# Position numbers behind a low part, five rows and three v tiles in flight, 33 u tiles ahead

## The chip, the cores and the metric

The kernel runs on one core of one Trainium2 chip. The metric is the device time of one execution in microseconds. Before the change it took 2081.49 us (median of 3 runs, 2076.62 to 2083.87).

## The reference

One layer each of two blocks over 512 tokens of width 1024, in float32. The first block (gated attention beside a gated delta rule) and the token mixers of the second (a linear recurrence beside a convolution) end at about 800 us of the profile and are not touched by the change. What the change touches is the last part, a product-key expert layer:

```python
q = (t @ w_q).reshape(n_tok, 8, 2, 128)              # 8 heads, 2 halves
sc = einsum("thpk,hpnk->thpn", q, sub_keys)           # 128 keys a half
s_top, i_top = top_k(sc, 16)                          # of each half
cand = s_top[:,:,0,:,None] + s_top[:,:,1,None,:]      # 16 x 16 pairs
best, pos = top_k(cand, 16); idx = cand_idx[pos]      # 16 experts a head
g = softmax(best)
act = gelu(einsum("phkd,pd->phk", u_tab[idx], t))     # 128 experts a token
out = einsum("phk,phkd->pd", g * act, v_tab[idx])     # of 16384 in the tables
```

The result is added to the residual, and a last rms norm follows.

## The kernel before, in words

Tokens stand on columns (512 of them) in the transposed layout, weights come as 128 x 1024 tiles. Float32 precision is had from pairs: a tile is cast to a rounded high part by ScalarE (`whi`, `vhi`, `xhi`, line 192) and the rest, the low part, is a subtraction on GpSimd or VectorE (`wlo`, `vlo`, `xlo`, line 193). Each product is three matmuls: high with high, low with high, high with low.

**Query stage** (`peer_query`). For each of 8 heads, two blocks of `wq` (one for each half, e = 0 and 1) are projected, scored against the keys (`scp`), and VectorE finds the 16 best of each half (`top16`, lines 1153 to 1157: `val`, `ind`). From the two sets of indices GpSimd makes the position numbers `f` (line 1054 from half 0, line 1055 from half 1), from them the candidates' indices `cidx` (line 1070); VectorE finds the 16 best pairs; then VectorE writes four masks `eq`, GpSimd multiplies each with `cidx` (`pr`, line 1096), and VectorE adds up (`idxf`, line 1097). Between the heads stand u tiles (`u_step`, line 988): two after each of the first seven heads and six after the last.

**u tiles and v tiles.** For 352 of the 512 tokens all 16384 experts are computed, 128 at a time. A u tile is 24 matmuls (`ups`), and its gelu is kept in a ring of `RUN` = 32 tiles (`act`). The v tile of the same number (18 matmuls into `acc`) comes `LAG` = RUN - 2 u tiles later, after the gate matrix (`gate_matrix`: one-hot matmuls `gp`, written to device memory as `gd`, read back as `gate` for four tiles at a time) has been multiplied into it (`act`, line 1317) and the product split into `ch` and `cl`. From u tile 20 on VectorE makes the low part of u; it makes those of v too.

**Rows.** The other 160 tokens gather their experts' rows: GpSimd issues an indirect DMA (line 1227) into one of `NROW` = 4 row buffers, and VectorE multiplies and sums each (lines 1233 and 1249). There are 160 rows of u and 160 of v, each 128 x 1024. They are paced by `spent`: 8 for each turn in which both a u and a v tile are done, 4 for a turn with a v tile alone, 324 steps over `total - 40`.

**What sets the order.** Instructions are recorded in the order of the code, and a scheduler puts them into each engine's queue; an engine then works through its queue in order. `tc.issue_after(ins)` holds the instructions of its block that are on `ins`'s engine behind `ins`. `vring` holds 4 v tiles in the buffer that was `xr`, which is free after its transposes into `acc` (line 1283). All loads but the rows go through SyncE's queue in order.

Of the kernel before, what the change touches and what calls it, by code (L numbers as in the profile page):

```python
# [6 lines left out]
F32 = mybir.dt.float32  # L7
# [5 lines left out]
OP = mybir.AluOpType  # L13
# [170 lines left out]
def vec(g, name, i, n=1):  # L184
    o, w = VEC[name]
    return g.vec[:, o + i:o + i + n]
# [15 lines left out]
def wblock(g, src, k=KD, width=128, lo_eng=None, ret=False, raw=None):  # L202
    nc = g.nc
    if raw is None:
        raw = wblock_load(g, src, k, width)
    hi = g.wp.tile([128, k, width], F32R, name="whi", tag="whi")
    lo = g.wp.tile([128, k, width], F32R, name="wlo", tag="wlo")
    last = split(g, hi, lo, raw, lo_eng or nc.gpsimd)
    return (hi, lo, last) if ret else (hi, lo)
# [15 lines left out]
def proj_tile(g, w, xhi, xlo, ks=range(KD), ps=None):  # L225

    if ps is None:
        ps = g.pmm.tile([128, 512], F32, name="mm", tag="mm")
    hi, lo = w
    mm3(g, ps, lambda k: hi[:, k, :], lambda k: lo[:, k, :], lambda k: xhi[:, k, :], lambda k: xlo[:, k, :], ks)  # L230
    return ps
# [744 lines left out]
TB = 32  # L976
GPAD = 128
NEXP = 128
RUN = 32
GB = 4  # L980
ULO = 20
NROW = 4
SMH = 4
UQ = [2, 2, 2, 2, 2, 2, 2, 6]
PM = 2


# [15 lines left out]
def peer_query(g, xr):  # L1003

    nc, tc = g.nc, g.tc
    V = nc.vector
    L = g.L
# [2 lines left out]
    g.xtok = {tt: L.tile([128, 1024], F32, name=f"xtok{tt}") for tt in GT}  # L1010
    g.xnt = {tt: L.tile([128, 1024], F32, name=f"xnt{tt}", tag=f"xnt{tt}") for tt in GT}
    g.xnx = L.tile([128, 1024], F32, name="xnx", tag="xnx")
    g.idxf = L.tile([128, 4, 128], F32, name="idxf")
    g.wgt = L.tile([128, 4, 128], F32, name="wgt")
    with ExitStack() as c2:
        P = c2.enter_context(tc.tile_pool(name="pq", bufs=1, reuse_waits="tile"))
        R = c2.enter_context(tc.tile_pool(name="pqr", bufs=2, reuse_waits="tile"))
# [9 lines left out]
        nx = P.tile([128, KD, len(DT) * 128], F32, name="nx")  # L1027
        for k in range(KD):
            V.scalar_tensor_tensor(nx[:, k, :], xr[:, k, cs], vec(g, "n2", k), g.rb[:, cs], op0=OP.mult, op1=OP.mult)
        for h in range(8):  # L1030
            val = R.tile([128, 4, 2, 16], F32, name="val")
            ind = R.tile([128, 4, 2, 16], U32, name="ind")
            for e in range(2):
                hp = 2 * h + e
                ps = proj_tile(g, wblock(g, g.a["wq"][hp]), g.xhi, g.xlo)
                if hp == 1:
                    for k in range(KD):
                        split(g, g.xhi[:, k, cs], g.xlo[:, k, cs], nx[:, k, :])
                qT = R.tile([128, T], F32, name="qT")
                nc.scalar.copy(qT, ps)  # L1040
                ps = pt.tile([128, 512], F32, name="scp", tag="pg")
                for tt in range(4):
                    nc.tensor.matmul(ps[:, tt * 128:(tt + 1) * 128], qT[:, tt * 128:(tt + 1) * 128], sk[:, hp, :],
                                     start=True, stop=True)
                sc = R.tile([128, 4, 128], F32, name="sc")
                for tt in range(4) if h == 0 else GT:
                    nc.scalar.activation(sc[:, tt, :], ps[:, tt * 128:(tt + 1) * 128], AF.Copy, scale=g.rtok[:, tt:tt + 1])
                if h:
                    nc.scalar.copy(sc[:, DT[0]:, :], ps.rearrange("p (t n) -> p t n", t=4)[:, DT[0]:, :])
                for tt in range(4):  # L1050
                    top16(g, R, val[:, tt, e, :], ind[:, tt, e, :], sc[:, tt, :])

            f = R.tile([128, 4, 2, 16], F32, name="f")
            nc.gpsimd.tensor_scalar(out=f[:, :, 0, :], in0=ind[:, :, 0, :], scalar1=128.0, scalar2=None, op0=OP.mult)
            nc.gpsimd.tensor_copy(f[:, :, 1, :], ind[:, :, 1, :])
            cand = R.tile([128, 4, NCAND], F32, name="cand")
            cidx = R.tile([128, 4, NCAND], F32, name="cidx")

            def pairs(eng, out, x, y, at, a, b, na, nb):

                o = out[:, :, at:at + na * nb]
                x, y = x[:, :, a:a + na], y[:, :, b:b + nb]
                if na > 1 and nb > 1:
                    s4 = [128, 4, na, nb]
                    o, x, y = o.rearrange("p t (a b) -> p t a b", b=nb), x[:, :, :, None].to_broadcast(s4), y[:, :, None, :].to_broadcast(s4)
                elif nb > 1:
                    x = x.to_broadcast([128, 4, nb])
                elif na > 1:
                    y = y.to_broadcast([128, 4, na])
                eng.tensor_tensor(out=o, in0=x, in1=y, op=OP.add)  # L1070

            for a in range(5):
                pairs(V, cand, val[:, :, 0, :], val[:, :, 1, :], START[a], a, 0, 1, START[a + 1] - START[a])
            pairs(V, cand, val[:, :, 0, :], val[:, :, 1, :], START[5], 5, 0, 3, 2)
            pairs(V, cand, val[:, :, 0, :], val[:, :, 1, :], START[8], 8, 0, 8, 1)
            at = 0
            for a, b, na, nb in RUNS:
                pairs(nc.gpsimd, cidx, f[:, :, 0, :], f[:, :, 1, :], at, a, b, na, nb)
                at += na * nb
            best = R.tile([128, 4, 16], F32, name="best")  # L1080
            pos = R.tile([128, 4, 16], U32, name="pos")
            for tt in range(4):
                top16(g, R, best[:, tt, :], pos[:, tt, :], cand[:, tt, :])
            pf = R.tile([128, 4, 16], F32, name="pf")
            V.tensor_copy(pf, pos)
            V.tensor_tensor(out=g.wgt[:, :, h * 16:h * 16 + 16], in0=best, in1=best[:, :, 0:1].to_broadcast([128, 4, 16]),
                            op=OP.subtract)
            for q, n in enumerate(ENDS):

                v4 = lambda t: t[:, :16 * n].rearrange("p (t k c) -> p t k c", t=4, k=4)  # L1090
                s4 = [128, 4, 4, n]
                eq = v4(R.tile([128, 16 * NCAND], BF16, name="eq"))
                V.tensor_tensor(out=eq, in0=rank[:, None, None, :n].to_broadcast(s4),
                                in1=pf[:, :, 4 * q:4 * q + 4, None].to_broadcast(s4), op=OP.is_equal)
                pr = v4(R.tile([128, 16 * NCAND], F32, name="pr"))
                nc.gpsimd.tensor_tensor(out=pr, in0=eq, in1=cidx[:, :, None, :n].to_broadcast(s4), op=OP.mult)  # L1096
                V.tensor_reduce(out=g.idxf[:, :, h * 16 + 4 * q:h * 16 + 4 * q + 4], in_=pr, axis=AX.X, op=OP.add)
            if h % SMH == SMH - 1:
                e = g.wgt[:, :, (h + 1 - SMH) * 16:(h + 1) * 16]
                e4 = e.rearrange("p t (h k) -> p t h k", k=16)  # L1100
                nc.scalar.activation(e, e, AF.Exp)
                l = R.tile([128, 4, SMH], F32, name="l")
                V.tensor_reduce(out=l, in_=e4, axis=AX.X, op=OP.add)
                V.reciprocal(l, l)
                V.tensor_tensor(out=e4, in0=e4, in1=l[:, :, :, None].to_broadcast([128, 4, SMH, 16]), op=OP.mult)
            for _ in range(UQ[h]):
                u_step(g)
        g.u_last = g.u_mm
        for n in range(0, KD, 4):
            for tt in GT:  # L1110
# [90 lines left out]
def peer_experts(g, out, xr, gd):  # L1201
    nc, tc = g.nc, g.tc
    V = nc.vector
    NB = ND // TB
    with ExitStack() as ctx:
# [16 lines left out]
        gx.dot = P.tile([128, GX], F32, name="dotx")  # L1222
        gat.insert(0, gx)

        def gather(s, tab, i):
            r = R.tile([128, 1024], F32, name="row", bufs=NROW)
            nc.gpsimd.indirect_dma_start(out=r, out_offset=None, in_=g.a[tab],  # L1227
                                         in_offset=bass.IndirectOffsetOnAxis(ap=s.idx[:, i:i + 1], axis=0))
            return r
# [26 lines left out]
        def finish(hs, tt):  # L1256

            ss = R.tile([128, 2], F32, name="ss")
            o = R.tile([128, 1024], F32, name="o", tag="row", bufs=NROW)
            half = [slice(e * 512, (e + 1) * 512) for e in range(2)]  # L1260
            sq = g.wp.tile([128, KD, 128], F32, name="wraw", tag="wraw").rearrange("p k d -> p (k d)")
            for e in range(2):
# [18 lines left out]
        for m, tt in enumerate(DT):  # L1281
            for k in range(KD):
                nc.tensor.matmul(acc[m][k // 4][:, (k % 4) * 128:(k % 4 + 1) * 128], xr[:, k, tt * 128:(tt + 1) * 128], g.ident,
                                 start=k % 4 == 0, stop=False)
        vring = g.xp.tile([128, 4, 1024], F32, name="vring", tag="xr")
        LAG = RUN - 2

        chl = [[P.tile([128, GX + ND], F32R, name=f"{n}{j}") for n in ("ch", "cl")] for j in range(2)]
# [12 lines left out]
                        nc.tensor.matmul(acc[m][e], l[:, ts], r[:, e * 512:(e + 1) * 512], start=False, stop=end and l is cl)  # L1301

        gt = None
        total = sum(8 if LAG <= n < NEXP else 4 for n in range(LAG, NEXP + LAG))
        spent = 0
        for n in range(NEXP + LAG):
            if n < NEXP:
# [10 lines left out]
                            in1=gt[:, :, i % GI, :], op=OP.mult)  # L1318
            ch, cl = chl[i % 2]
            split(g, ch[:, GX:], cl[:, GX:], act)  # L1320
            vr = vring[:, i % 4, :]
            nc.sync.dma_start(vr, g.a["v"][i * 128:(i + 1) * 128, :])
            vh = R.tile([128, 1024], F32R, name="vhi")
            vl = R.tile([128, 1024], F32R, name="vlo")
# [9 lines left out]
                    products([m])  # L1334
            if i != NEXP - 2:
                late.clear()
            spent += 8 if n < NEXP else 4
            with tc.issue_after(last.ins):
                while done < min(len(steps), len(steps) * spent // (total - 40)):
                    f, s, i = steps[done]  # L1340
# [41 lines left out]
```

## Time and profile before

| | |
|---|---|
| profiled execution | 2073.55 us |
| its span, first to last instruction | 2071.8 us |
| median of 3 runs | 2081.49 us |
| TensorE (PE) busy | 1992.9 us, 96% |
| VectorE (DVE) busy | 1554.4 us, 75% |
| GpSimd (POOL) busy | 1028.6 us, 50% |
| ScalarE (ACT) busy | 838.0 us, 40% |
| DMA | 423.43 MB, 204 GB/s over the span |

A share of busy time is a mean over stages. In the profile's 40 slices the DMA engines are in the nines from slice 23 on (about 1140 us), where u tiles, v tiles and rows run together, and low before. Idle time of TensorE is 78.9 us of the span in all; where it lies, and what ended it, is what has to be read.

### The profile page before, as it was taken

To read this page: it belongs to the slowest core of one execution; us is meant where nothing else is said; L and a number is where in the kernel's file an instruction comes from. 1 tells how busy PE (TensorE), PEld (TensorE's weight loads), DVE (VectorE), ACT (ScalarE), POOL (GpSimd) and SP (SyncE) were. 2 spreads that over 40 slices of the span, in tenths; PEclk is the share of its full clock that TensorE was granted. 3 is DMA by queue.
4 is the path that set the end of the run, shared out by engine and by line. 5 is a ranking of instruction groups with operands and counts; after the bars stand their busy time and mean duration, and the time that the engine had idled before them with its cause. 6 is when DMAs were issued, how large, how long until landed. Compare 5 with 4: busy or idle time off the path is not lost.

```text
span 2071.8 us, 28916 instructions
## 1 busy us (share of the span) xinstructions
PE 1992.9 (96%) x10588; PEld 1722.8 (83%) x10588; DVE 1554.4 (75%) x2647; ACT 838.0 (40%) x1337; POOL 1028.6 (50%) x876
## 2 busy tenths in 40 slices
PE   9999999899999999988999898999999999999997
PEld 6787887677888877877899787899989898989885
DVE  6635545367777778888898789898888888888683
ACT  5444444444444444333454333333333333333343
POOL 3544352345666555667677454454444444545330
PEclk9999999999999999999999999999999999999999
DMA  4111121312222233222366999999999999998682
GB/s 163 55 38 42 67 77 51 102 63 91 92 90 93 92 99 105 89 85 92 112 245 264 375 356 362 374 383 375 347 358 359 347 353 359 340 367 314 231 286 81
DMA packets 152125, 423.43 MB, mean 204 GB/s; under 512 B 12592, under 2 KB 57776, under 8 KB 150320
## 3 DMA queue, kind: packets, MB, share of 16 engines
q1 hardware_dynamic: 105904, 253.80, 35.1%
q0 software_dynamic: 46080, 167.79, 22.2%
q8 instruction: 83, 1.36, 0.3%
q14 instruction: 58, 0.48, 0.1%
HBM read 396.38 MB, written 25.17 MB: 203 GB/s over the span
## 4 chain that ended last, share of the span: by engine, by line
PE 42%; DVE 8%; issue 4%; POOL 4%; DMA 3%; ACT 0%; SPq 0%; POOLq 0%; DVEq 0%; ACTq 0%
PE acc L1301 22%; PE ups L217 16%; PE gp L1195 2%; POOL row L1227 2%; DMA gate<-gd 1%; PE mm L217 1%; DVE oh L1189 1%; DVE t L1155 1%; POOL pr L1096 1%; DMA row<-v,ix 1%; DVE ind L1154 1%; DVE ind L1157 1%; POOL oh L1191 1%; DVE val L1153 1%; DVE val L1156 1%
## 5 line engine op out<-in xcount | busy, mean ns | idle before, releaser
L193 POOL TENSOR_TENSOR wlo<-wraw,whi 128x1024 fp32r<-128x1024 f32 x136 | 334.9, 2467 | 219.4 <-ACT whi L192 215.8
L192 ACT CAST whi<-wraw 128x1024 fp32r<-128x1024 f32 x248 | 258.8, 1044 | 88.4 <-issue 31.8
L1227 POOL DMA_INDIRECT row<-v,idx x128 | 166.4, 1300 | 191.7 <-DVE xtok L1249 167.6
L1301 PE MATMUL acc<-vlo,ch 128*128 128x512 f32 x768 | 240.3, 393 | 9.6 <-DVE vlo L193 9.5
L1227 POOL DMA_INDIRECT row<-u,idx x128 | 157.7, 1232 | 179.1 <-DVE row L1233 163.4
L1301 PE MATMUL acc<-vhi,ch 128*128 128x512 f32 x768 | 240.2, 393 | 3.9 <-ACT ch L192 3.9
L1301 PE MATMUL acc<-vhi,cl 128*128 128x512 f32 x768 | 240.3, 394 | 0.0
L217 PE MATMUL mm<-xhi,wlo 128*128 128x512 f32 x824 | 221.4, 399 | 8.7 <-POOL wlo L193 8.7
L217 PE MATMUL mm<-xhi,whi 128*128 128x512 f32 x824 | 221.9, 402 | 4.3 <-DVE bb L863 3.7
L217 PE MATMUL mm<-xlo,whi 128*128 128x512 f32 x824 | 220.1, 399 | 0.0
L217 PE MATMUL ups<-xhi,whi 128*128 128x352 f32 x1024 | 197.2, 327 | 1.2 <-ACT act L999 1.2
L217 PE MATMUL ups<-xhi,wlo 128*128 128x352 f32 x1024 | 190.9, 326 | 7.2 <-POOL wlo L193 5.0
L217 PE MATMUL ups<-xlo,whi 128*128 128x352 f32 x1024 | 193.3, 327 | 1.7 <-DVE xlo L193 1.6
L192 ACT CAST ch<-act 128x352 fp32r<-128x352 f32 x128 | 62.4, 487 | 319.3 <-PE acc L1301 280.1
L999 ACT ACTIVATE act<-ups 128x352 f32<-128x352 f32 x128 | 59.4, 464 | 307.6 <-PE ups L217 307.6
L217 PEld LDWEIGHTS mm<-xhi,wlo 128*128 128x128 f32 x824 | 150.5, 189 | 39.4 <-POOL wlo L193 11.2
L1301 PEld LDWEIGHTS acc<-vlo,ch 128*128 128x128 f32 x768 | 144.0, 188 | 45.5 <-DVE vlo L193 13.9
L217 PEld LDWEIGHTS mm<-xhi,whi 128*128 128x128 f32 x824 | 148.9, 189 | 37.1 <-issue 9.2
L217 PEld LDWEIGHTS ups<-xhi,whi 128*128 128x128 f32 x1024 | 170.2, 189 | 11.2 <-ACT act L999 1.5
L217 PEld LDWEIGHTS mm<-xlo,whi 128*128 128x128 f32 x824 | 151.5, 189 | 30.8 <-issue 2.1
L217 PEld LDWEIGHTS ups<-xhi,wlo 128*128 128x128 f32 x1024 | 168.1, 190 | 9.2 <-POOL wlo L193 6.5
L1249 DVE SCALAR_TENSOR_TENSOR xtok<-row,dot,xtok 128x1024 f32<-128x1024 f32 x128 | 163.9, 1280 | 13.0 <-DMA row<-v,idx 11.5
(642 smaller groups left out, 3740.5 us busy)
## 6 DMA issues: line engine op xcount, KB each, us to landing
wraw<-uT SPq DMA_DIRECT2D x128, 512.0 KB, 6.5
vring<-v SPq DMA_DIRECT2D x128, 512.0 KB, 6.8
wraw<-w SPq DMA_DIRECT2D x88, 512.0 KB, 3.4
gd<-stage SPq DMA_DIRECT2D x11, 2048.0 KB, 7.2
gate<-gd SPq DMA_DIRECT2D x32, 704.0 KB, 9.4
wraw<-wo SPq DMA_DIRECT2D x16, 512.0 KB, 3.4
wraw<-wq SPq DMA_DIRECT2D x16, 512.0 KB, 3.5
xr<-xT SPq DMA_DIRECT2D x8, 256.0 KB, 6.6
```

Source lines behind the costliest of these rows:

```text
L192: nc.scalar.copy(hi, src)
L193: return (lo_eng or nc.vector).tensor_tensor(out=lo, in0=src, in1=hi.bitcast(F32), op=OP.subtract)
L217: yield nc.tensor.matmul(out, w(k), x(k), start=j == 0, stop=j == len(ps) - 1)
L999: nc.scalar.activation(act, ups, AF.Gelu_apprx_tanh)
L1096: nc.gpsimd.tensor_tensor(out=pr, in0=eq, in1=cidx[:, :, None, :n].to_broadcast(s4), op=OP.mult)
L1153: V.max(out=v[:, 0:8], in_=x)
L1154: V.max_index(out=i[:, 0:8], in_max=v[:, 0:8], in_values=x)
L1155: V.match_replace(out=y[:, :n], in_to_replace=v[:, 0:8], in_values=x, imm_value=-3.0e38)
L1195: nc.tensor.matmul(ps[:, j * 128:(j + 1) * 128], oh[:, 1, j, :], oh[:, 0, j, :], start=True, stop=True)
L1227: nc.gpsimd.indirect_dma_start(out=r, out_offset=None, in_=g.a[tab], in_offset=bass.IndirectOffsetOnAxis(ap=s.idx[:, i:i + 1], axis=0))
L1249: V.scalar_tensor_tensor(s.acc, r, s.dot[:, i:i + 1], s.acc, op0=OP.mult, op1=OP.add)
L1301: nc.tensor.matmul(acc[m][e], l[:, ts], r[:, e * 512:(e + 1) * 512], start=False, stop=end and l is cl)
```

## The change

Five things change together. The u tiles of a head and the next head's first `wq` block now stand in the code ahead of the position numbers, and these are held behind the last low part among them. There are five row buffers: four tiles of their own and the fourth slot of `vring`, so that the v tiles have three slots. The ring of u tiles has 33 places, for which `idxf` has moved into another buffer. The pace is 0 in the first two turns with a v tile.

```diff
-RUN = 32
+RUN = 33
+VR = 3
...
-NROW = 4
+NROW = 5
...
-UQ = [2, 2, 2, 2, 2, 2, 2, 6]
+UQ = [2, 2, 2, 2, 2, 2, 2, 3]
+UEND = 3
...
-    g.idxf = L.tile([128, 4, 128], F32, name="idxf")
+    g.idxf = g.hp.tile([128, 4, 128], F32, name="idxf", tag="rb")
...
+        wq = [wblock(g, g.a["wq"][0], ret=True)]
...
-                ps = proj_tile(g, wblock(g, g.a["wq"][hp]), g.xhi, g.xlo)
+                ps = proj_tile(g, (wq.pop(0) if wq else wblock(g, g.a["wq"][hp], ret=True))[:2], g.xhi, g.xlo)
...
+            for _ in range(UQ[h]):
+                last = u_step(g)
+            if h < 7:
+                wq.append(wblock(g, g.a["wq"][2 * h + 2], ret=True))
+                last = wq[0][2]
...
-            nc.gpsimd.tensor_scalar(out=f[:, :, 0, :], in0=ind[:, :, 0, :], scalar1=128.0, scalar2=None, op0=OP.mult)
-            nc.gpsimd.tensor_copy(f[:, :, 1, :], ind[:, :, 1, :])
+            with tc.issue_after(last.ins):
+
+                nc.gpsimd.tensor_scalar(out=f[:, :, 0, :], in0=ind[:, :, 0, :], scalar1=128.0, scalar2=None, op0=OP.mult)
+                nc.gpsimd.tensor_copy(f[:, :, 1, :], ind[:, :, 1, :])
...
-            for _ in range(UQ[h]):
-                u_step(g)
+        for _ in range(UEND):
+            u_step(g)
...
+        vring = []
+        rows = [P.tile([128, 1024], F32, name=f"row{j}") for j in range(NROW - 1)]
+        turn = [0]
+
+        def row():
+            turn[0] += 1
+            return (rows + [vring[0][:, VR, :]])[turn[0] % NROW]
+
         def gather(s, tab, i):
-            r = R.tile([128, 1024], F32, name="row", bufs=NROW)
+            r = row()
...
-        vring = g.xp.tile([128, 4, 1024], F32, name="vring", tag="xr")
+        vring.append(g.xp.tile([128, VR + 1, 1024], F32, name="vring", tag="xr"))
...
-        total = sum(8 if LAG <= n < NEXP else 4 for n in range(LAG, NEXP + LAG))
+        pace = lambda n: 0 if n < LAG + 2 else 8 if n < NEXP else 4
+        total = sum(map(pace, range(LAG, NEXP + LAG)))
...
-            vr = vring[:, i % 4, :]
+            vr = vring[0][:, i % VR, :]
...
-            spent += 8 if n < NEXP else 4
+            spent += pace(n)
```

GpSimd's queue at the third head's position numbers, before (`wlo` are low parts of weight blocks: the last of a head's two u tiles, then the next head's two `wq` blocks):

```order
L1096 TENSOR_TENSOR pr<-eq,cidx 128x800
L193 TENSOR_TENSOR wlo<-wraw,whi 128x1024
L1054 TENSOR_SCALAR f<-ind 128x4x16
L193 TENSOR_TENSOR wlo<-wraw,whi 128x1024 x2
L1055 CAST f<-ind 128x4x16
L1070 TENSOR_TENSOR cidx<-f 128x4x4
```

The same place of the changed kernel:

```order
L1106 TENSOR_TENSOR pr<-eq,cidx 128x800
L193 TENSOR_TENSOR wlo<-wraw,whi 128x1024 x2
L1064 TENSOR_SCALAR f<-ind 128x4x16
L193 TENSOR_TENSOR wlo<-wraw,whi 128x1024
L1065 CAST f<-ind 128x4x16
L1080 TENSOR_TENSOR cidx<-f 128x4x4
```

One low part, that of the next head's first `wq` block, now stands ahead of `f`. The low part of the last u tile ahead of it still stands behind the head's largest `pr`. At the other heads but the first it is the same move; no other engine's queue changes in this stage.

TensorE's queue where the first v tile begins, before (`acc` are the v tiles' sums; u tile 32 is the one that is split):

```order
L217 MATMUL ups<-xhi,whi 128x352 x8
L217 MATMUL ups<-xhi,wlo 128x352 x6
L1301 MATMUL acc_9676<-vhi,ch_9707 128x512
L1301 MATMUL acc_9677<-vhi,ch_9707 128x512
L1301 MATMUL acc_9676<-vlo,ch_9707 128x512
```

And now:

```order
L217 MATMUL ups<-xhi,whi 128x352 x8
L217 MATMUL ups<-xhi,wlo 128x352
L1319 MATMUL acc_9680<-vhi,ch_9711 128x512
L1319 MATMUL acc_9681<-vhi,ch_9711 128x512
L1319 MATMUL acc_9680<-vlo,ch_9711 128x512
```

The first v tile begins five u matmuls earlier, inside the same u tile. Before, v tiles 0 and 1 followed on each other there; now the rest of u tile 32 stands between them, and from v tile 2 on each v tile k has 32 + k whole u tiles ahead of it, where it had 31 + k.

VectorE's queue from the low part of v tile 10 to that of v tile 11, before (`row` and `accx` rows are gathered rows):

```order
L193 TENSOR_TENSOR vlo<-vring,vhi 128x1024
L1237 TENSOR_TENSOR dotx<-dotx,wx 128x32
L1241 MEMSET accx 128x1024
L1317 TENSOR_TENSOR act<-act,gate 128x352
L1249 SCALAR_TENSOR_TENSOR accx<-row,dotx,accx 128x1024
L193 TENSOR_TENSOR wlo<-wraw,whi 128x1024
L1249 SCALAR_TENSOR_TENSOR accx<-row,dotx,accx 128x1024
L1317 TENSOR_TENSOR act<-act,gate 128x352
L193 TENSOR_TENSOR cl_9710<-act,ch_9709 128x352
L1249 SCALAR_TENSOR_TENSOR accx<-row,dotx,accx 128x1024
L193 TENSOR_TENSOR vlo<-vring,vhi 128x1024
```

And now:

```order
L193 TENSOR_TENSOR vlo<-vring,vhi 128x1024
L1251 SCALAR_TENSOR_TENSOR row_9676,dotx<-row_9676,xnx 128x1024
L1336 TENSOR_TENSOR act<-act,gate 128x352 x5
L193 TENSOR_TENSOR wlo<-wraw,whi 128x1024
L1251 SCALAR_TENSOR_TENSOR row_9677,dotx<-row_9677,xnx 128x1024
L1251 SCALAR_TENSOR_TENSOR row_9678,dotx<-row_9678,xnx 128x1024
L193 TENSOR_TENSOR cl_9714<-act,ch_9713 128x352
L193 TENSOR_TENSOR vlo<-vring,vhi 128x1024
```

The gate products that run ahead of the v tiles have moved forward: counted from the first, 29 stand ahead of the low part of v tile 11 now, 13 before, beside 32 rows now and 35 before. The fifth of the five in one row is the first that needs the next gate block.

## Rows read from the trace of the kernel before

**Rows 1.** Busy time of engines by stretch: PE, PEld, DVE, ACT, POOL, PEclk, DMA, GB/s.

```profile
1133.00:1340.00 207.00, 191.33 (x976) 167.54 (x975) 171.66 (x234) 70.12 (x102) 95.22 (x71) 0.98 1.02 367
1340.00:2057.00 717.00, 717.00 (x3687) 639.04 (x3686) 595.70 (x741) 264.16 (x369) 308.08 (x247) 1.00 0.91 326
```

**Rows 2.** Waits of TensorE from 800 to 1012 us: total, times, longest.

```profile
PE mm L217 <- POOL wlo L193: 8.7, 6, 1.9
PE ups L217 <- POOL wlo L193: 5.0, 5, 2.4
```

**Rows 3.** Timeline of GpSimd from 848 us: start, us, instruction, idle before.

```profile
852.32 2.42 POOL L193 TENSOR_TENSOR wlo<-wraw,whi 128x1024 fp32r<-128x1024 f32 x1
858.58 0.37 POOL L1054 TENSOR_SCALAR f<-ind 128x64 f32<-128x64 uint32 x1 [3.85 <-DVE ind L1157]
858.92 4.72 POOL L193 TENSOR_TENSOR wlo<-wraw,whi 128x1024 fp32r<-128x1024 f32 x2
...
875.71 2.41 POOL L193 TENSOR_TENSOR wlo<-wraw,whi 128x1024 fp32r<-128x1024 f32 x1
```

**Rows 4.** Timeline of TensorE from 848 us.

```profile
878.17 1.54 PE L217 MATMUL ups<-xhi,wlo 128*128 128x352 f32 x8 [0.21 <-POOL wlo L193]
...
884.68 2.85 PE L217 MATMUL mm<-xhi,wlo 128*128 128x512 f32 x8 [1.87 <-POOL wlo L193]
```

**Rows 5.** Waits of TensorE from 1133 to 1340 us.

```profile
PE acc L1301 <- DVE vlo L193: 9.5, 7, 2.2
PE acc L1301 <- ACT ch L192: 3.9, 1, 3.9
PE ups L217 <- DVE wlo L193: 2.1, 1, 2.1
```

**Rows 6.** Chain that ended last, 1120 to 1140 us: start, us, piece.

```profile
1127.62 9.96 DMA gd<-stage
```

**Rows 7.** Nine earlier writes of `gd`, 1010 to 1115 us.

```profile
DMA to landing us min/median/max: 6.3/7.2/8.5
```

**Rows 8.** Timeline of SyncE's queue from 1100 us.

```profile
1137.65 0.38 SPq L1316 DMA_DIRECT2D gate<-gd  x1
```

**Rows 9.** Timeline of VectorE and TensorE at the first v tile.

```profile
1146.25 0.52 DVE L1317 TENSOR_TENSOR act<-act,gate 128x352 f32<-128x352 f32 x1 [0.86 <-DMA gate<-gd]
...
1147.35 0.73 PE L1301 MATMUL acc<-vhi,ch 128*128 128x512 f32 x2 [3.93 <-ACT ch L192]
```

**Rows 10.** Timeline of VectorE from 1254 us.

```profile
1255.88 1.39 DVE L1317 TENSOR_TENSOR act<-act,gate 128x352 f32<-128x352 f32 x3
1257.18 1.22 DVE L193 TENSOR_TENSOR wlo<-wraw,whi 128x1024 fp32r<-128x1024 f32 x1
1258.32 1.28 DVE L1249 SCALAR_TENSOR_TENSOR accx<-row,dotx,accx 128x1024 f32<-128x1024 f32 x1
1259.52 0.52 DVE L1317 TENSOR_TENSOR act<-act,gate 128x352 f32<-128x352 f32 x1
```

**Rows 11.** Waits of VectorE from 1140 to 1244 us.

```profile
DVE row L1233 <- DMA row<-u,ix: 13.9, 10, 2.7
...
DVE accx L1249 <- DMA row<-v,ix: 2.3, 1, 2.3
```

**Rows 12.** Timeline of TensorE from 1300 us: a v tile and a u tile.

```profile
1317.89 0.63 PE L1301 MATMUL acc<-vhi,ch 128*128 128x512 f32 x2
...
1322.03 1.43 PE L217 MATMUL ups<-xhi,whi 128*128 128x352 f32 x8
...
1325.83 0.63 PE L1301 MATMUL acc<-vhi,ch 128*128 128x512 f32 x2
```

**Rows 13.** DMA from 1140 to 1340 us: packets, MB, share; then issues, KB, landing.

```profile
q1 hardware_dynamic: 27367, 36.40, 54.1%
q0 software_dynamic: 10089, 36.75, 48.1%
...
gate<-gd SPq DMA_DIRECT2D x14, 704.0 KB, 10.0
```

**Rows 14.** Loads of v tiles from 1925 to 2057 us, where no u tile is left.

```profile
DMA to landing us min/median/max: 3.4/5.1/7.3
```

More of the change, by code (lines that the diff above doesn't have):

```diff
@@ L1258, in finish @@
             ss = R.tile([128, 2], F32, name="ss")
-            o = R.tile([128, 1024], F32, name="o", tag="row", bufs=NROW)
+            o = row()
             half = [slice(e * 512, (e + 1) * 512) for e in range(2)]
```

## The prediction

> **What bounds the kernel now.** I read the busy time by stretch first, then who waited for whom in the two stretches where TensorE is not full, then the timelines there. From 1340 to 2057 us TensorE is busy 717.00 of 717 us [rows 1]: nothing that the change does to other engines can win there, it can only lose. From 1133 to 1340 us it is busy 191.33 of 207 us, and the waits name 15.5 us: 3.9 for the first `ch`, 2.1 for a low part of u, 9.5 in seven waits for low parts of v [rows 5]. DMA moves 367 GB/s in that stretch against 326 in the next [rows 1]. In the query stage, 800 to 1012 us, TensorE waits 8.7 + 5.0 = 13.7 us for GpSimd's low parts [rows 2]. The matmuls are the same in both kernels, so the time changes by what these idle times do, as far as TensorE's later work is not held by something else anyway.
>
> **Query stage: nothing.** The reader should see the knot on GpSimd's queue in [rows 3]: the u tile's low part ends at 854.7, then GpSimd sits 3.85 us in `f`, which waits for VectorE's indices, and two `wq` low parts of 2.36 us each run only behind it. The change puts the first of them into that gap. 2.4 us fit into 3.85, so `f` is not late, and the second low part comes 2.4 us earlier too. The wait of 1.87 us at 884.68 [rows 4] is of this kind and goes; longest is 1.9 [rows 2]. But what is late next is the low part of the head's second u tile. It stands behind the largest `pr`, and that waits for VectorE's mask, at the end of VectorE's chain for the head. It starts at 852.32 and again at 875.71: a head takes 23.4 us by VectorE's pace [rows 3]. TensorE reached that low part at 877.96 and waited 0.21 [rows 4]. If it comes there 1.9 us earlier, it waits 2.1 us instead. No queue of VectorE changes here and the `pr` keep their places, so the head takes 23.4 us as before, and the stage ends where it ended. Cost 0. On the loss side the margin is 3.85 - 2.4 = 1.4 us a head, and the low part's cast is done one block ahead, so I leave no loss; on the gain side the bound is the whole 13.7 us, a rival below. Moving `idxf` into the old `rb` buffer costs nothing: VectorE reads `rb` last and writes `idxf` first, in order. The new places of the u tiles in the code leave TensorE's queue here as it was.
>
> **First v tile: -2.0 us.** Its matmuls waited 3.93 us, from 1143.42 to 1147.35, and ran 1.10 us after the gate block had landed at 1146.25 [rows 9]. That block was asked for at 1137.65 [rows 8], as soon as the last `gd` write had landed, 9.96 us after its start [rows 6]. Nine writes before it took 7.2 in the median [rows 7]; the last one shared the engines with four row gathers. Now the first gather goes into `vring`, which is free only after the transposes (1133 us), and stands first in GpSimd's queue. So the write has the engines to itself until then: it lands 2.8 us earlier, the gate block at about 1143.6 with the same 8.6 us, and the v tile can begin at 1144.6. TensorE is there at 1142.6, five matmuls earlier than before (5 x 0.16, a u tile being 3.80 us for 24 [rows 12]). Wait 2.0 instead of 3.9. Bounds: no wait at all, or 4.7 us if the write gains nothing.
>
> **The low part of u: -2.1 us.** That wait stood behind nine passes over rows that now come later: with no rows in the first two turns VectorE does four gate products, two `cl` and the low part at once (about 3.7 us by the steps of [rows 10]), and TensorE has more than a v tile to do meanwhile. Bounds 0 and -2.1.
>
> **The low parts of v: -2.5 us.** For it: one more u tile, 3.80 us of TensorE's work [rows 12], lies ahead of each v tile from the third on. Against it: VectorE's queue has moved the gate products forward. By the steps of [rows 10] a row takes 1.20 us, a low part 1.14, a gate product or `cl` 0.43. From the first gate product to the low part of v tile 11 there now stand 32 rows (38.4), 29 gate products (12.5), 11 low parts of u (12.5), 10 of v (11.4) and 12 `cl` (5.2): 80.0 us, so 1223.6 without any stall. TensorE wants that low part after 11 v tiles of 4.14 and 10.6 u tiles of 3.80 [rows 12], 1144.6 + 45.5 + 40.3 + 0.5 = 1230.9. VectorE's stalls decide. Up to its twelfth v tile they were 13.9 + 2.3 us for rows [rows 11]. The first of these fall away with the first rows, and a fifth buffer lets a row be asked for earlier; but the engines are as full as before. I keep 10. The fifth gate product in the row of five needs a block that is asked for only when the one before it has been multiplied: 3 us of VectorE's work into the turn, and landing takes 10.0 [rows 13], against 11.2 us of work up to it, so 1.8 us more. 1223.6 + 11.8 = 1235.4, and TensorE waits 4.5 us there. Up to v tile 16 a gate block still comes with each turn, and I add 2.5 us for that: 7.0 in place of 9.5. Bounds: with no stalls 0, with all 16.2 us (and the 1.8) 10.7 + 2.5 = 13.2.
>
> **Steady part: 0.** Rows go at 324 x 8 / 844 = 3.07 a turn instead of 3.00, 0.09 us more for VectorE, which is idle for 717 - 595.7 us, and for DMA at 326 GB/s [rows 1]. If that cover were gone it would cost 95 x 0.09 = 8 us. Three slots for v: below.
>
> **Sum.** 2.0 + 2.1 + 2.5 = 6.6 us less. The profiled execution took 2073.55 us, span 2071.8 and 1.75 around it, so 2067.0 for such a one; it lies 7.9 us below the median of the runs, and taken off that the forecast is 2074.9. With all the lucky ends 2.0 + 1.9 + 2.1 + 9.5 = 15.5, with the unlucky ones (4.7 and 13.2, the low part of u as before) 4.5 more: 2066.0 to 2086.0.
>
> **Rivals.**
> (a) *The lead is eaten by the loads.* In [rows 13] SyncE's queue (q1) and GpSimd's (q0) moved 36.40 and 36.75 MB: half each. In the turns of v tiles 7 to 16 SyncE's queue has a u tile, a v tile and a gate block to bring, 0.524 + 0.524 + 0.721 = 1.77 MB, and at half of 367 GB/s that takes 9.6 us for a turn of 7.94. Ten turns cost 17 us, less 3.8 for the lead: 13, and with 2.0 for the first v tile that is the 15.5 of before. Time 2081. It needs a row queue that never runs dry, which five buffers make likelier; against it, not every such turn waited before. The Trainium skill, "DMA: Bandwidth & Descriptors", "Queues, rings and completion order", says that each DMA engine serves the queues that have work in turn. By that a fifth row in flight cannot take more than half from the v tiles, but keeps it always; the halves of the trace agree.
> (b) *All waits of 1133 to 1340 go*, and with them TensorE's half-speed stretches there (granted clock 0.98 of 207 us [rows 1], up to 4 us): 15.5 + 4 = 19.5, time 2062. For it: the u tile more and the rows held back. Against it: the gate products in front.
> (c) *The query waits really go.* If TensorE rather than VectorE set the pace of a head, the 8.7 us of `wq` waits [rows 2] would go as well: 2066. Against it: 23.4 us from low part to low part [rows 3], with TensorE waiting once in each.
> (d) *Slower: three slots for v tiles are too few where only v tiles are left.* A v tile's load starts when the low part three tiles earlier is done. At 4.14 us a tile that leaves 12.4 us, less about 2.3 for cast and subtraction: 10.1. With four slots it was 14.2. Loads there land in 5.1, at most 7.3 us [rows 14], so there is room; from 10.1 us on, every tile is late. If the rows that now reach further into this part, five deep, bring landing to 10.6, 31 tiles lose 0.5 each, 15.5, net of the 6.6 a loss of 8.9: 2090.
>
> **Chances.** Forecast 0.45 (its own range 2070 to 2080), (a) 0.20, (b) 0.12, (c) 0.08, (d) 0.15. About 0.3%, 6.2 us, is what a measurement of this kernel can tell from no change. The forecast lies just beyond that line and gives 0.25 to faster and 0.20 to same; (b) and (c) are faster; (a) is same but for 0.03; (d) gives 0.12 to slower and 0.03 to same. Faster 0.45, same 0.40, slower 0.15. The range 2063 to 2087 takes in the bounds of the sum and leaves out most of (d) and the far end of (b).
>
> **What would show it.** Right: waits for GpSimd's low parts before 1012 us still 10 us or more, now at `ups` and hardly at `mm`; the last `gd` write landing in some 7 us; no row pass ahead of the low part of u tile 33; one long wait for `vlo` near v tile 11 and small ones up to 16; none after 1340. Wrong: a head of the query stage shorter than 23 us; the first v tile beginning at 1147 or later; `vlo` waits of more than 12 us in all, or of less than 3; any wait for `vlo` or `vhi` after the last u tile.

## The result, and the profile after

The changed kernel took 2068.37 us in the median of 5 runs (2059.74 to 2069.85), the kernel before 2083.87 in runs beside it (2076.62 to 2088.97). The ratio is 0.9931 with a 95% interval of 0.9903 to 0.9959: 14 us faster, between 9 and 20. The profiled execution took 2068.37 us, span 2066.6. It ran 20.5 us at half clock near 204 us, in a part that the change doesn't touch, and reached the matmul into `rank`, with which the query stage begins, at 799.1 us instead of 788.3. So I compare from `rank` on, by three stretches of TensorE in one profiled execution of each kernel: A from `rank` to the last `gp` matmul, B from there to the first v product, C from there to the last one.

| us | A | B | C | sum |
|---|---|---|---|---|
| before | 338.4 | 20.7 | 910.4 | 1269.5 |
| after | 334.2 | 18.6 | 900.8 | 1253.6 |
| difference | -4.2 | -2.0 | -9.7 | -15.9 |

The busy time by stretch, the answer to [rows 1] (PE, PEld, DVE, ACT, POOL, PEclk, DMA, GB/s):

```profile
1133.00:1340.00 207.00, 198.11 (x1055) 179.75 (x1053) 175.44 (x239) 72.67 (x106) 104.38 (x74) 0.98 1.03 378
1340.00:2057.00 717.00, 713.01 (x3668) 635.62 (x3667) 598.24 (x748) 263.81 (x373) 334.39 (x251) 1.00 0.90 328
```

TensorE is busy 198.1 of 207 us where it was 191.3; the second window now reaches 4 us past its last product. Its waits from 800 to 1012 us, against [rows 2]:

```profile
PE ups L217 <- POOL wlo L193: 4.9, 4, 1.8
PE scp L1046 <- ACT qT L1043: 4.6, 1, 4.6
```

and from 1133 to 1340 us, against [rows 5]:

```profile
PE acc L1319 <- DVE vlo L193: 6.7, 1, 6.7
PE acc L1319 <- ACT ch L192: 2.2, 1, 2.2
```

The `mm` waits are gone and those at `ups` did not take their place: 4.9 us for low parts where it was 13.7. Other waits came instead, 4.6 us for `qT` and 3.2 for `act`, so that the waits that the profile lists from 780 to 1030 us fell only from 19.8 to 17.9 us. The wait for a low part of u is gone, and seven waits for `vlo` have become one.

**A: VectorE stood still inside an instruction.** GpSimd's queue in one head, against [rows 3] (start, us, instruction, idle before):

```profile
868.40 0.37 POOL L1064 TENSOR_SCALAR f<-ind 128x64 f32<-128x64 uint32 x1 [1.47 <-DVE ind L1167]
868.74 2.41 POOL L193 TENSOR_TENSOR wlo<-wraw,whi 128x1024 fp32r<-128x1024 f32 x1
873.55 0.35 POOL L1065 CAST f<-ind 128x64 f32<-128x64 uint32 x1 [2.41 <-DVE ind L1167]
```

One low part stands between the two halves of `f` where there were two, and GpSimd has 2.41 us to spare. VectorE meanwhile, first before, then after (`cand` is the sum of two value lists, two additions to a row):

```profile
861.79 0.27 DVE L1156 MAX8 val<-t 128x8 f32<-128x128 f32 x1
...
862.57 0.27 DVE L1155 MATCH_REPLACE8 t<-val,sc 128x128 f32<-128x128 f32 x1
862.76 1.01 DVE L1070 TENSOR_TENSOR cand<-val 128x32 f32<-128x32 f32 x2
863.70 0.28 DVE L1156 MAX8 val<-t 128x8 f32<-128x128 f32 x1
```

```profile
872.39 0.27 DVE L1165 MATCH_REPLACE8 t<-val,sc 128x128 f32<-128x128 f32 x1
872.58 0.27 DVE L1080 TENSOR_TENSOR cand<-val 128x32 f32<-128x32 f32 x2
872.77 0.29 DVE L1166 MAX8 val<-t 128x8 f32<-128x128 f32 x1
```

The same two additions take 1.01 us and 0.27. In [rows 3] the two low parts end at 858.92 + 4.72 = 863.64, and the first addition ends 0.04 us later. The first `cand` addition of a head lasts 0.88 to 1.01 us in seven heads of eight before, each time until 0.04 to 0.06 us after a low part's end, and 0.18 to 0.19 in seven of eight after. The searches of VectorE beside the same low parts (`MAX8` at 861.79 and `MATCH_REPLACE8` at 862.57, one tile read) keep their 0.27 us. From one head's `idxf` additions to the next head's it takes 22.5 to 22.6 us instead of 23.3 to 23.4 in five of the seven steps, 21.4 instead of 22.1 in the first, and 26.2 in both kernels in the step to the fifth head. From the first `idxf` addition to the last it is 166.6 us instead of 171.3.

The Trainium skill, "SBUF — State Buffer", section "Who interferes with whom", has the rule: a VectorE instruction with two inputs in SBUF contends with a GpSimd instruction that reads SBUF, and the one that starts first keeps the shared ports until it ends. The rows agree: 0.9 us for the addition with two inputs, no change for the searches with one.

**B.** SyncE's queue, DVE and PE at the first v tile, against [rows 6, 8, 9]:

```profile
1134.14 0.32 SPq L1207 DMA_DIRECT2D gd<-stage  x1
1141.96 0.38 SPq L1335 DMA_DIRECT2D gate<-gd  x1
```

```profile
1150.73 1.40 DVE L1336 TENSOR_TENSOR act<-act,gate 128x352 f32<-128x352 f32 x3 [2.68 <-DMA gate<-gd]
```

```profile
1151.83 0.73 PE L1319 MATMUL acc<-vhi,ch 128*128 128x512 f32 x2 [2.16 <-ACT ch L192]
```

The last `gd` write took 7.8 us instead of 10.0, the gate block another 8.8, and the wait is 2.16 instead of 3.93.

**C.** SyncE's queue and VectorE at the one long wait, then TensorE, against [rows 10]:

```profile
1227.29 0.38 SPq L1335 DMA_DIRECT2D gate<-gd  x1
```

```profile
1231.96 1.83 DVE L1336 TENSOR_TENSOR act<-act,gate 128x352 f32<-128x352 f32 x4 [0.95 <-DMA gate<-gd]
1240.80 0.52 DVE L1336 TENSOR_TENSOR act<-act,gate 128x352 f32<-128x352 f32 x1 [7.01 <-DMA gate<-gd]
```

```profile
1239.03 0.62 PE L1319 MATMUL acc<-vhi,ch 128*128 128x512 f32 x2
1246.38 1.22 PE L1319 MATMUL acc<-vlo,ch 128*128 128x512 f32 x2 [6.72 <-DVE vlo L193]
1247.40 1.06 PE L1319 MATMUL acc<-vhi,cl 128*128 128x512 f32 x2
```

The fifth gate product of that turn stood 7.0 us for its block, which had been asked for at 1227.29 and landed 13.5 us later, and TensorE stood 6.7 us behind it. Then two products took 1.06 us instead of 0.62: the granted clock fell to the lower of its two levels, 1.2 GHz, at 1244.90, 1.5 us before the wait ended, and stayed there for 6.8 us.

Waits explain 4.9 of the 9.7 us in C (2.1 + 9.5 before, 6.7 now). Most of the rest is a pitch. A turn of a u tile and a v tile took 7.94 us in [rows 12] and takes 7.90 now:

```profile
1606.07 0.63 PE L1319 MATMUL acc<-vhi,ch 128*128 128x512 f32 x2
...
1613.97 0.40 PE L1319 MATMUL acc<-vhi,ch 128*128 128x512 f32 x1
```

A v product starts 227.8 ns after the one before it instead of 229.8 in the mean from 1400 to 1900 us, without any wait; the first nine of a turn's 18 steps and the last one are the slower ones. 0.04 us in 96 turns are 3.8 us. On the other side, C holds 10.2 us at the lower clock now and held 6.8 before; what is left of the 9.7 was not traced.

### The profile page after: what moved, and what is told of

It is laid out like the page before. It is cut to its first block, busy times and chain, and to the rows that moved or that the text cites. A ratio compares the mean times of both kernels' runs of the same rounds, so it can differ in the third digit from the quotient of the medians.

```text
span 2066.6 us, 28848 instructions
## 1 busy us (share of the span) xinstructions
PE 1996.3 (97%) x10588; PEld 1735.7 (84%) x10588; DVE 1553.3 (75%) x2647; ACT 837.6 (41%) x1337; POOL 1059.2 (51%) x876
## 4 chain that ended last, share of the span: by engine, by line
PE 43%; DVE 9%; DMA 4%; POOL 3%; issue 2%; ACT 0%; POOLq 0%; SPq 0%; DVEq 0%; ACTq 0%
PE acc L1319 23%; PE ups L217 16%; PE gp L1205 2%; DMA gate<-gd 2%; DVE oh L1199 1%; DVE t L1165 1%; POOL pr L1106 1%; DVE ind L1164 1%; DVE ind L1167 1%; DMA wraw<-uT 1%; DVE val L1163 1%; DVE val L1166 1%; DVE idxf L1107 1%; POOL oh L1201 1%; POOL wlo L193 0%
## 5 line engine op out<-in xcount | busy, mean ns | idle before, releaser
L217 PE MATMUL mm<-xhi,whi 128*128 128x512 f32 x824 | 226.4, 408 | 3.7 <-DVE bb L863 3.7
L1245 POOL DMA_INDIRECT row<-v,idx x102 | 138.4, 1357 | 129.9 <-DVE xtok L1267 113.4
L217 PE MATMUL ups<-xhi,whi 128*128 128x352 f32 x1024 | 198.1, 329 | 3.2 <-ACT act L1001 3.2
L1245 POOL DMA_INDIRECT row<-u,idx x103 | 133.9, 1300 | 127.7 <-DVE row L1251 109.4
L217 PEld LDWEIGHTS ups<-xhi,whi 128*128 128x128 f32 x1024 | 170.8, 190 | 12.6 <-ACT act L1001 3.5
L193 DVE TENSOR_TENSOR wlo<-wraw,whi 128x1024 fp32r<-128x1024 f32 x112 | 137.7, 1233 | 46.2 <-ACT whi L192 46.0
```

The lines of the kernel that those rows point to most:

```text
L193: return (lo_eng or nc.vector).tensor_tensor(out=lo, in0=src, in1=hi.bitcast(F32), op=OP.subtract)
L217: yield nc.tensor.matmul(out, w(k), x(k), start=j == 0, stop=j == len(ps) - 1)
```

## The experiments

Each is compared by the three stretches; the ratio is that to the kernel before, run beside it.

| kernel | A | B | C | v pitch, ns | ratio (95%) |
|---|---|---|---|---|---|
| reorder alone | 335.6 | 19.8 | 909.4 | 229.8 | 0.9945 (0.9923 to 0.9967) |
| reorder undone | 340.0 | 17.7 | 900.7 | 227.8 | 0.9929 (0.9902 to 0.9955) |
| one more subtraction | 340.1 | 17.4 | 902.7 | 227.8 | 0.9961 (0.9940 to 0.9982) |
| old buffers | 334.2 | 16.3 | 904.6 | 227.8 | 0.9903 (0.9876 to 0.9929) |
| rows at once | 333.1 | 21.7 | 897.7 | 227.8 | 0.9943 (0.9921 to 0.9964) |
| lead of 33 alone | 339.2 | 20.3 | 901.1 | 227.8 | 0.9970 (0.9951 to 0.9989) |
| products spread | 333.2 | 17.5 | 890.1 | 227.8 | 0.9862 (0.9840 to 0.9884) |
| spread, old buffers | 335.9 | 15.8 | 894.7 | 227.8 | 0.9872 (0.9849 to 0.9895) |
| spread, exp later | 329.7 | 18.8 | 890.2 | 227.8 | 0.9854 (0.9833 to 0.9876) |
| spread, lead of 32 | 332.8 | 22.3 | 895.4 | 229.8 | one run |
| spread, lead of 31 | 334.2 | 21.2 | 898.4 | 227.8 | one run |

A scatters where the query stage is the same: from 332.8 to 335.9 us in the eight kernels with the new order (without the subtraction and with the exponential in its place), and the time at half clock in it, 13.7 to 20.5 us, does not put them in order. The time from the first `idxf` addition of VectorE to the last scatters far less: 171.3 to 171.5 us in the three kernels with the old order (before, reorder undone, lead alone), 166.6 to 166.8 in those eight.

**Reorder alone**, in the kernel before (with the `u_step` calls and the next `wq` block moved ahead of it, as in the change):

```
- nc.gpsimd.tensor_scalar(out=f[:, :, 0, :], ...)
+ with tc.issue_after(last.ins):
+     nc.gpsimd.tensor_scalar(out=f[:, :, 0, :], ...)
...
```

> The kernel before with the reordered GpSimd queue of the query stage alone. Three stretches on TensorE are read: A from the `rank` matmul to the last `gp` (338.4 us before, 334.2 after), B from there to the first v product (20.7 and 18.6), C from there to the last one (910.4 and 900.8). Theory P: in the kernel before VectorE's first `cand` addition of a head lasts 0.9 us because it stands still until a low part that GpSimd is running ends; with a low part less between the two `f` it lasts 0.18. Then seven heads have a `cand` of 0.18, a head takes 22.6 us instead of 23.4, A is 334 +- 1, B and C are as before, and the time is about 4 us below that of before. Rival R: the 4 us in A came with the rest of the change (u tiles, `idxf` in another buffer): A stays at 338.

**Reorder undone**: these lines taken back in the changed kernel.

> The changed kernel with the old order of GpSimd's query stage, all else kept. Theory P: the first `cand` addition lasts 0.9 us again in seven of eight heads, a head takes 23.4 us, A is 338 +- 1, while B (18.6) and C (901) stay as in the changed kernel: about 4 us more than it. Rival R: A stays at 334. If the steady pitch of u and v turn (7.94 us before, 7.90 after) is tied to the query part in any way, C grows by 3 us; I expect no tie.

The two additions of the third head, with the reorder alone, then with it undone:

```profile
861.52 0.28 DVE L1080 TENSOR_TENSOR cand<-val 128x32 f32<-128x32 f32 x2
```

```profile
874.74 0.99 DVE L1070 TENSOR_TENSOR cand<-val 128x32 f32<-128x32 f32 x2
```

The first addition follows the queue both ways. With the reorder alone it takes 0.18 to 0.19 us in seven heads and a head 22.6; undone, 0.89 to 0.98 in seven heads and 23.4. The time from the first `idxf` addition to the last goes with it, 166.7 and 171.5 us. From `rank` on the reorder alone gives 4.6 us, and undoing it costs 4.8. A itself came out longer than I expected in both, 335.6 (334 +- 1) and 340.0 (338 +- 1). R has fallen. The times of whole executions are too coarse for it: the reorder alone is 7 to 16 us faster than the kernel before, and with it undone the ratio is that of the whole change, 0.9929 against 0.9931.

**One more subtraction**, with no one waiting for it:

```
+ wq.append(wblock(g, g.a["wq"][2 * h + 3], ret=True))
+ with tc.issue_after(wq[1][2].ins):
+     nc.gpsimd.tensor_tensor(out=g.xnx[:, :768], in0=<768 of nx>, in1=<val[:, 3, 1, 0:1]>, op=OP.subtract)
```

> The changed kernel with one more GpSimd subtraction a head, 128x768 with both inputs in SBUF, into a buffer that nobody reads at that time, placed behind the low part that stands between the two `f` and ahead of the second `f`, where GpSimd is idle for 2.4 us. No one waits for its result and no low part comes later. Theory P: it runs about 1.8 us, from 0.9 us before VectorE's first `cand` addition on, and that addition stands still until it ends: about 0.95 us instead of 0.18, a head takes 23.3 us instead of 22.6 in some six heads, A is 338 to 339, the time 4 to 5 us above the changed kernel's. Rival Q: what made the heads shorter is that TensorE no longer waits for the low parts of `wq`, and VectorE's `cand` has no part in it: A stays at 334, the probe is free.

GpSimd and VectorE in one head of it:

```profile
874.04 2.40 POOL L193 TENSOR_TENSOR wlo<-wraw,whi 128x1024 fp32r<-128x1024 f32 x1
877.08 1.47 POOL L1062 TENSOR_TENSOR xnx<-nx,val 128x768 f32<-128x768 f32 x1 [0.64 <-DVE val L1167]
879.39 0.29 POOL L1069 CAST f<-ind 128x64 f32<-128x64 uint32 x1 [0.84 <-DVE ind L1171]
```

```profile
877.89 0.80 DVE L1084 TENSOR_TENSOR cand<-val 128x32 f32<-128x32 f32 x2
878.61 0.28 DVE L1170 MAX8 val<-t 128x8 f32<-128x128 f32 x1
```

The subtraction ends at 878.55, and the addition lasts until then: 0.71 us instead of 0.18. It ran 1.47 us and not 1.8, so a head takes 23.15 us and not 23.3, in four steps. In the first head the second addition stood too, 1.49 us, and the step to the fifth head grew from 26.2 to 27.6, which was not traced; so A is 340.1, above the 338 to 339 that I expected. P holds and Q falls: nothing on TensorE waits for this subtraction, and from the first `idxf` addition to the last it is 171.0 us again.

**Old buffers**:

```
- VR = 3
- NROW = 5
...
- return (rows + [vring[0][:, VR, :]])[turn[0] % NROW]
+ VR = 4
+ NROW = 4
...
+ return rows[turn[0] % NROW]
```

> The changed kernel with the buffers of before: four slots for v tiles, four for rows, no row in the v ring; reorder, 33 u tiles and the held-back rows stay. Two things are open. Steady pitch: if the row in the v ring or the three v slots made the turn 7.90 us instead of 7.94, it is 7.94 again and C grows by 3 us; if it comes from the later phase of VectorE against TensorE, it stays at 7.90. Lead: if the fifth row matters for the wait near v tile 11, TensorE waits more than 6.7 us there (up to 10, VectorE's stalls for rows being 4 us longer); if the gate block alone decides it, 6.7 +- 1. B: with no row in the v ring the first gathers can start at 1133 us beside the last `gd` write; they are held back by VectorE's queue, not by GpSimd's, so if it was the buffer that kept the write alone, B is 20 again, otherwise 18.6.

The pitch stays at 227.8, so the buffers do not set it. The fifth row is a trade: without it VectorE waited 24 us for rows up to v tile 24 (6 with it), and TensorE 9.1 us for four low parts, at most 2.9 at a time: the long wait at v tile 11, which I expected at 6.7 or more, did not come. But the first gather began 1.0 us after the first gate block was asked for and not 2.0 us ahead of it, and the first v product had no wait. My expectation for B was wrong in the good direction.

**Rows at once**:

```
- pace = lambda n: 0 if n < LAG + 2 else 8 if n < NEXP else 4
+ pace = lambda n: 8 if n < NEXP else 4
```

> The changed kernel without holding the rows back: they are spread from the first v tile on, as before. Two things are read. The start: VectorE has row passes ahead of the first gate products again, so the low part of u tile 33 is late once more (2 us waited in the kernel before), and B is 19 to 21. The steady pitch: 18 v products take 227.8 ns each in the changed kernel and 229.8 before, 3 us in all; if it is the number of rows a turn (3.07 instead of 3.00) or where in the turn VectorE runs the row passes, this kernel falls back to 229.8; if it is the lead of one u tile, it stays at 227.8. I expect the fall back with 0.6.

VectorE ahead of the first gate product, and TensorE behind it:

```profile
1135.27 1.23 DVE L1251 SCALAR_TENSOR_TENSOR vring<-vring,xnx 128x1024 f32<-128x1024 f32 x1 [3.06 <-DMA vring<-u,ix]
...
1139.67 1.23 DVE L1251 SCALAR_TENSOR_TENSOR row<-row,xnx 128x1024 f32<-128x1024 f32 x1 [2.03 <-DMA row<-u,ix]
```

```profile
1143.04 1.22 PE L1319 MATMUL acc<-vhi,ch 128*128 128x512 f32 x2 [4.98 <-ACT ch L192]
```

B is 21.7 and the wait for `ch` 5.0 us, though the last `gd` write landed in 7.8 us here too: VectorE stood 3.06 and 2.03 us for rows ahead of the gate product. So B needs both, the write alone and no row pass in front. C is 3 us shorter than with the rows held back, so holding them back gained nothing in sum (1252.5 us from `rank` on, 1253.6 in the changed kernel). The low part of u tile 33 was not late, as I had expected it to be. The fall back in pitch, which I had expected with 0.6, did not come.

**Lead of 33 alone**, in the kernel before:

```
- RUN = 32
- g.idxf = L.tile([128, 4, 128], F32, name="idxf")
+ RUN = 33
+ g.idxf = g.hp.tile([128, 4, 128], F32, name="idxf", tag="rb")
```

> The kernel before with 33 u tiles ahead alone (and `idxf` in the other buffer for it). The lead is worth one u tile, 3.80 us of TensorE's work, ahead of each v tile from the third on: the waits for `vlo` from 1133 to 1340 us fall from 9.5 to 5 or 6 if VectorE only lags, and stay near 9 if its lag grows by stalls. A stays at 338, B at 20.7. Steady pitch: 229.8 ns a v product if the held-back rows set it, 227.8 if the lead does.

```profile
PE acc L1301 <- DVE vlo L193: 6.3, 5, 2.4
```

C falls by 9.3 us, nearly the whole gain of the change there: 6.3 us of waits for `vlo` instead of 9.5, no wait for a low part of u, where it was 2.1, and the pitch of 227.8.

**Spread, lead of 32 and of 31**, in the kernel with spread products below:

```
- RUN = 33
+ RUN = 32   (then 31)
```

> The kernel with the spread gate products, with 32 u tiles ahead instead of 33 (`idxf` stays in its new buffer). Only the pitch of the v products from 1400 to 1900 us is read. Theory L: the lead sets it (33 ahead 227.8 ns, with and without the rest of the change, 32 ahead 229.8): 229.8 here. Rival I: the moved `idxf`, and with it the places of other tiles in SBUF, sets it: 227.8 here.

> The same with 31 u tiles ahead. If an odd number makes the faster pitch (buffers that take turns two by two then fall in another way on u and v tiles), it is 227.8 ns here; if the faster pitch needs a long lead, 229.8 or more. I hold odd and even for likelier, 0.6.

Turns with 32 ahead (7.94 us), then with 31 (7.90):

```profile
1605.77 0.63 PE L1319 MATMUL acc<-vhi,ch 128*128 128x512 f32 x2
...
1613.71 0.63 PE L1319 MATMUL acc<-vhi,ch 128*128 128x512 f32 x2
```

```profile
1607.25 0.63 PE L1319 MATMUL acc<-vhi,ch 128*128 128x512 f32 x2
...
1615.15 0.63 PE L1319 MATMUL acc<-vhi,ch 128*128 128x512 f32 x2
```

With a lead of 31 or 33 the pitch is 227.8 ns, with one of 32 it is 229.8, in all of the kernels here. The moved `idxf` does not make it (rival I has fallen), nor a long lead. That it is odd against even is the likeliest reading, but 32 is the only even lead that was run, and which of the buffers that take turns would make it was not tried: the cause of the pitch is open.

**Products spread**: product i stands behind the low part of v tile i-4.

```
- V.tensor_tensor(out=act..., in1=gt[:, :, i % GI, :], op=OP.mult)
+ with tc.issue_after(lows[max(i - 4, 0)].ins) if i >= 4 else nullcontext():
+     V.tensor_tensor(out=act..., in1=gt[:, :, i % GI, :], op=OP.mult)
...
  x = split(g, vh, vl, vr)
+ lows.append(x)
```

> The changed kernel with the gate products held back: product i of VectorE stands behind the low part of v tile i-4, one a turn instead of four or five. Theory G: the one long wait of the changed kernel (7.1 us at the low part of v tile 11) is the fifth product of a turn, for which VectorE stood 7.0 us until its gate block landed; blocks then came every turn, 0.72 MB each, and VectorE had four products a turn. With one product a turn a block is wanted every fourth turn: no wait for `vlo` of more than 1 us, stretch C (first to last v product, 900.8 us) 893 +- 2, A and B as in the changed kernel, time about 7 us below it. Rival H: it was the row passes and the load of the DMA engines; VectorE then waits for rows instead, `vlo` waits of 4 us or more stay and C is 898 or more.

TensorE from 1133 to 1340 us, its waits and its busy time:

```profile
PE acc L1319 <- ACT ch L192: 1.1, 1, 1.1
```

```profile
1133.00:1340.00 207.00, 205.92 (x1091) 185.80 (x1090) 177.91 (x233) 78.43 (x113) 106.53 (x80) 1.00 1.01 379
```

No wait for a low part is left, nor a stretch at half clock. C fell by 10.7 us, more than the 8 or so that I expected and than the 6.7 us of the wait, since 10.2 us at half clock went with it. At 2049.07 us it beats both kernels. VectorE waits 2.3 us for gate blocks instead of 12.6, and 6.9 for rows where it was 6.3: H has fallen.

**Spread, old buffers**: both edits together.

> The same with the buffers of before (four v slots, four rows). With these buffers the first v product came without any wait for `ch` (B 16.3 us instead of 18.6), since the first gather started after the first gate block was asked for; but VectorE waited 24 us for rows instead of 6 up to v tile 24, and C was 904.6. Theory G: with the gate blocks spread the DMA engines have room (about 0.5 MB a turn less), rows land sooner, C is 894 to 897, B 16.3, and the time is 1 to 2 us below the kernel with five rows. Rival H: rows stay late with four buffers, C 900 or more.

B came as expected. C is within its range, but TensorE waited 2.7 us for a low part, since VectorE stood 23 us for rows, and B and C together are 2.9 us longer than with five rows, where I expected the whole to be 1 to 2 us shorter. The ratios of the two can't be told apart.

**Spread, exp later** (`qc` is the last query copy into `qT`; the sum, the reciprocal and the product that VectorE makes of the exponentials move with them):

```
- if h % SMH == SMH - 1:
-     nc.scalar.activation(e, e, AF.Exp)
+ if h in (SMH, 7):
+     with tc.issue_after(qc.ins):
+         nc.scalar.activation(e, e, AF.Exp)
```

> The kernel with the spread gate products, with the exponential of the first four heads' weights moved on ScalarE behind the last query copy of the fifth head. In the changed kernel that head takes 26.2 us instead of 22.6: ScalarE's queue holds the exponential, which waits for the fourth head's weights, ahead of the query copy that TensorE waits 4.6 us for. Theory: with the exponential behind it that head takes 22.6 to 23.5 us, A falls by 3 to 3.6 us, and the time is about 3 us below the kernel with spread products alone (2049 us). Rival: VectorE's chain holds the fifth head anyway and A stays within 1 us.

The fifth head fell only from 26.2 to 25.3 us, but the sixth from 22.6 to 20.4: 3.1 us of the two, as expected in sum. The 4.6 us for `qT` are gone, but TensorE's waits for low parts rose from 4.2 to 7.2 us and that for `act` from 3.2 to 4.7. The 3 us can't be seen in the times (2047.2 against 2049.1 us, ranges overlapping).

## Why the prediction was right, and where it was not

The forecast was 2074.9 us, a gain of 6.6; measured were 2068.4 in the median and 15.9 us in the stages. The time lies in the range of 2063 to 2087, but the gain is more than twice the forecast one: two terms that I held at 0 were not 0, and one of the three others came out right by luck.

**First v tile, -2.0: right**, by its own steps: write 7.8 us (7.2 expected), wait 2.16 (2.0). The step left out that no row pass may stand ahead of the product; that was so here.

**Low part of u, -2.1: right in size.** No such wait is left. That the rows come later is not shown to be the cause: with the lead alone and with the rows at once the wait is gone too.

**Low parts of v, -2.5: right in sum (-2.8), wrong in parts.** The place was right, the fifth product and v tile 11. Of VectorE's stalls up to there I kept 10 us for rows and 1.8 for the gate block. They were 3.0 + 1.1 = 4.1 us for rows and, without the 2.7 us ahead of the first product, 9.9 for gate blocks:

```profile
DVE act L1336 <- DMA gate<-gd: 12.6, 5, 7.0
DVE row L1251 <- DMA row<-u,ix: 3.0, 3, 2.0
DVE vring L1251 <- DMA vring<-u,ix: 1.1, 1, 1.1
```

The block landed in 13.5 us where I took 10.0 from [rows 13]. So the wait was 6.7 instead of 4.5, near it because one term was too large and the other too small, and the 2.5 us of small ones up to tile 16 did not come. That the sum was right is luck. That the long wait let VectorE get ahead is likely, but was not tried.

**Query stage, 0: wrong, -4.2.** The step that failed is "No queue of VectorE changes here and the `pr` keep their places, so the head takes 23.4 us as before". VectorE's order did not change, but the duration of one of its instructions did. I had read GpSimd's 4.72 us from 858.92 in [rows 3] as work that lies beside VectorE's, and not laid VectorE's rows of those microseconds next to it. The wait was not moved to the second u tile, since VectorE's chain came 0.8 us a head sooner. The prediction's own sign of being wrong, a head shorter than 23 us, was there. Rival (c), with 8.7 and 2066, had the sign and came nearer to the time, but not the cause: the `mm` waits went as it said, other waits of TensorE took most of their place, and TensorE did not set the pace.

**Steady part, 0: wrong, -3 us.** The step was "nothing that the change does to other engines can win there, it can only lose": I took TensorE's busy time for time that it needs. Its 717 of 717 us [rows 1] held 0.04 us a turn, in 74 turns, that a lead of 33 gives back.

Of the rivals, (a) did not come: VectorE's waits for rows up to v tile 11 fell from 16.2 us [rows 11] to 4.1. The equal halves that (a) reads from [rows 13] are of bytes; they are 27367 packets on one queue and 10089 on the other, so they do not show equal turns. (b) did not come in the changed kernel; with the products spread 1.1 us of its waits are left and no half clock. (d) did not come: no wait for `vlo` or `vhi` after the last u tile, with three slots. From `rank` on the reorder alone gave 4.6 us and the lead alone 8.9; 2.4 of the 15.9 are left for rows and buffers, and neither is shown to gain: from `rank` on the old buffers cost 1.5 us, and with the rows at once it is 1.1 us less.

## What to carry to other kernels

Before a chain is called the bound of a stage, lay the other engines' rows of the same microseconds beside each of its instructions: one that lasts longer than its twins and ends with another engine's instruction is a wait that no list of waits shows. Work that a scheduler pulls forward because its inputs are there (here five gate products a turn) also pulls its transfers forward, into the stretch where the DMA engines are full; hold it to the pace at which it is used. And a lead between two loops that share buffers in turns can change the pitch by one place more or less: try the neighbours.

## What the hardware showed that I had not expected

VectorE's addition with two inputs stood still 0.7 us beside GpSimd's subtraction, inside its own duration (0.92 instead of 0.18 us), while its searches ran on at 0.28. TensorE's v products went at 229.8 ns with a lead of 32 and at 227.8 with 31 or 33, with no wait and the same clock. And a wait can cost more than its length: the 6.7 us at v tile 11 came with 6.8 us at 1.2 GHz, 5.3 of them after it, and where it was taken away no stretch of C ran at that clock.
